# Four row tiles of the last chunk of K in seven products, and the product units one place earlier

## The chip, the core and the metric

The kernel runs on one core of a Trainium2 chip. The core has a matrix engine (TensorE, PE in the profile, with its weight loads as PEld), a vector engine (DVE), a scalar engine (ACT), GpSimd (POOL), SyncE (SP), and 16 DMA engines that bring data from HBM. Measured is the device time of the one launch in microseconds (us).

## The reference

Two layers of an encoder over 256 positions of width 2048, in float32. Layer 0 mixes by pooling and grouped-query attention, layer 1 by an mLSTM; these parts are not touched. Behind each stands a gated feed-forward part, in which the change lies:

```python
def conv_ffn(x, w_up, conv_w, conv_b, w_down):      # D_FF = 5632
    u = x @ w_up                                     # 2048 -> 2 * 5632
    up = jnp.pad(u, ((0, 0), (1, 1), (0, 0)))
    u = c[0] * up[:, :-2] + c[1] * up[:, 1:-1] + c[2] * up[:, 2:] + conv_b
    gate, val = jnp.split(u, 2, axis=-1)
    return (jax.nn.silu(gate) * val) @ w_down        # 5632 -> 2048
...
    x = x + conv_ffn(rms_norm(x, norm_ffn[layer]), w_up[layer], conv_w[layer], conv_b[layer], w_down[layer])
```

## The kernel before

**Numbers.** Every float32 operand of a product is split in a high part, rounded to the matrix engine's fp32r type, and a low part that holds the rest. A product of two tiles is three matmuls: high by high, high by low, low by high (`product`, `mov_part`).

**Weights.** `Stream` feeds them in the order in which TensorE uses them. A tile of 128 x 1024 (512 KB) is loaded by SP into one of six buffers w; ACT casts its high part (L127) and DVE subtracts for the low part (L128), both into one of four buffers hl. A tile of hl serves 12 matmuls of a direct product, six of the seven-product kind, 16 of the up-projection. Some weights of the seven products are sums of two blocks: SP loads one, POOL adds the other by DMA (L109 to L113, tile sum, prepared up to ten tiles ahead), and a third is made by DVE from a load and that sum (L123, L124).

**Up.** The hidden width of 5632 is 44 tiles. `up` makes one tile of gate and one of value in 64 matmuls, and then: ACT copies out of PSUM (L427) and DVE adds (L428, tb_up), DVE multiplies by the norm (L984), ACT forms three terms of the convolution for each of the two (L989 to L991), DVE adds them (L992, L993), ACT takes the silu (L997), DVE multiplies (L998, tile s), ACT and DVE split the result into g (L999, L1000).

**Down.** K, the 5632 rows, goes in six chunks of 4, 8, 8, 8, 8 and 8 row tiles. The 2048 columns are four blocks of 512; blocks 0 and 1 are the first half (h = 0), 2 and 3 the second (h = 1). In all chunks but the last, two row tiles, two position tiles and the two blocks of a half are a 2 x 2 block product that is made in seven products in place of eight. For this, `combine` ("mix" in the plan) makes, for pair j of chunk c, three combinations of s into s3 and a fourth into s1: DVE steps L1006, L1007, L1008 (tile sf), then ACT casts (L1012) and DVE subtracts (L1013). Unit A takes four of the products (three with s3, one with g), unit B the other three (two with g, one with s1); a unit of two pairs has 24 or 18 matmuls (pp). `drain` adds a unit's sums out of PSUM to acc and x (L1068), and `total` finishes a half in eight adds (L1085) when its last unit is in. In layer 0, chunk 1 takes the seven products in the second half alone, pair by pair, and goes directly in the first.

The last chunk goes directly (dn, end): `down_two` takes blocks 0 and 1, row tiles 0 to 5 of both and then 6 and 7 of both; `down` takes blocks 2 and 3, in layer 1 the last of them in `down_end`. DVE adds each block to x (L437, L1114). In layer 0 each finished block goes to the next norm (`nxt.add`), whose transposes (xt, L315) open the mixer of layer 1; in layer 1 it goes out.

**Order.** TensorE's order is written by hand: `_ffn_plan` lists ups, units, mixes and downs, and each unit stands between two ups. DVE, ACT, POOL and SP have an order that the scheduling layer sets when the program is built; on the chip each works its own list in order. In the names below up1_36 is tile 36 of layer 1, the first of its chunk 5; s31_4_3 is s3 of layer 1, chunk 4, pair 3. Chunk c's units of both halves follow the ups of chunk c + 1:

```python
        if halves == (0, 1):
            slots = [[(kind, c - 1, h, js)] for h in (1, 0) for kind in "AB"
                     for js in ((0, 1), (2, 3))[: pairs // 2]]
...
        for i in range(n):
            seq.append(("up", c, i))
            seq += slots[i] if i < len(slots) else []
```

Of the kernel before, what the change touches and what calls it, by code (L numbers as in the profile page):

```python
# [16 lines left out]
P = 128  # L17
# [192 lines left out]
def trunk(ctx: ExitStack, tc: tile.TileContext, gx, xT, xn, call, catt, cml, weights, mixes, out):  # L210
# [749 lines left out]
    def ffn_layer(layer, norm, nxt):  # L960
        with ExitStack() as es:
# [7 lines left out]
            combos, pss, quads, seen = {}, {}, {}, set()  # L969
# [86 lines left out]
            def drain(kind, c, h, order):  # L1056

                x00, x01, x10, _ = parts_of_x(h)
                if kind == "A":
                    steps = [(acc[:, h, k], v.tensor_add, e) for k, e in enumerate(order[:3])]  # L1060
                    steps.append((x10, v.tensor_add, 3))
                else:
                    steps = [(acc[:, h, 3], v.tensor_add, 0), (x00, v.tensor_add, 1), (x01, v.tensor_sub, 2)]
                for to, op, e in steps:
                    if e in (4, 6, 5, 0) and (kind, h) not in seen:
                        a.copy(to, pss[e])
                    else:
                        tc.keep_in_program_order(op(to, to, pss[e]))  # L1068
# [47 lines left out]

            def down(c, b):
                gt, last = gts[c], c == len(FCH) - 1
                kts = list(range(FCH[c]))
                if last and nxt is None and b == NB - 1:  # L1120
                    down_end(gt, b, kts)
                    return
# [7 lines left out]
                elif last:  # L1130
                    nxt.add(b)

            def down_two(c):

                gt, n = gts[c], FCH[c]
                pss2 = [mmp.tile([P, 2, 512], F32, tag="mm", name=f"dn{layer}_{c}_{b}") for b in range(2)]
                for kts in (range(n - 2), range(n - 2, n)):
                    for ps in pss2:
                        mov_part(ps, lambda k: gt[:, k], list(kts), kts[0] == 0, kts[-1] == n - 1)
                wv.until(lambda: ("A", 0) not in seen or ("total", 0) in pss)  # L1140
                for b, ps in enumerate(pss2):
# [8 lines left out]
            for kind, c, i, *j in _ffn_plan(layer):  # L1150
# [7 lines left out]
                elif kind == "down":  # L1158
                    down(c, i)
                elif kind == "two":  # L1160
                    down_two(c)
# [23 lines left out]
def _mov(w):  # L1185

    return w.reshape(-1, 2, P, 512).transpose(0, 2, 1, 3).reshape(-1, P, CH * P)
# [38 lines left out]

def _halves(layer, c):

    return () if c in (-1, len(FCH) - 1) else (0, 1) if c in BOTH[layer] else (1,)


def _ffn_plan(layer):

    seq = []
    for c, n in enumerate(FCH):
        pairs = FCH[c - 1] // 2 if c else 0  # L1240
        halves = _halves(layer, c - 1)

        if halves == (0, 1):
            slots = [[(kind, c - 1, h, js)] for h in (1, 0) for kind in "AB"
                     for js in ((0, 1), (2, 3))[: pairs // 2]]
            slots = [[]] * (pairs < 4) + slots
        else:
            slots = [[(kind, c - 1, 1, (j,))] for kind in "AB" for j in range(pairs)]
            for b in range(2 if pairs else 0):
                slots[(b + 1) * pairs // 2 - 1].append(("down", c - 1, b))  # L1250

        busy = {j: k for k, slot in enumerate(slots) for u in slot if u[0] == "A" for j in u[3]}
        for i in range(n):
            seq.append(("up", c, i))
            seq += slots[i] if i < len(slots) else []
            if c < len(FCH) - 1:
                seq += [("mix", c, j) for j in range(n // 2) if i == max(2 * j + 1, busy.get(j, 0))]
    return seq + [("two", len(FCH) - 1, 0)] + [("down", len(FCH) - 1, b) for b in range(2, NB)]


def _down_chunks(layer, w):
# [2 lines left out]
    out, k0 = [], 0  # L1264
    for c, n in enumerate(FCH):
        rows = w[k0 * P : (k0 + n) * P]
        blocks = [_mov(rows[:, b * 512 : b * 512 + 512]) for b in range(NB) if b // 2 not in _halves(layer, c)]
# [18 lines left out]
def _ffn_weights(layer, up, parts):  # L1286
# [3 lines left out]
    for kind, c, i, *j in _ffn_plan(layer):  # L1290
# [1 line left out]
            out += up[u : u + 4]  # L1292
            u += 4
        elif kind in ("down", "two"):
            out += [next(down) for _ in range(FCH[c] // 2 * (2 if kind == "two" else 1))]
# [119 lines left out]
```

## Time and profile before

| | |
|---|---|
| time, median of 3 runs | 2163.98 us (2162.7 to 2164.5) |
| the profiled execution | 2163.78 us, span 2162.0 us |
| granted TensorE clock | 1.00 |
| DMA moved | 555.29 MB, mean 257 GB/s |
| largest groups of DVE and ACT | L128, 840 times, 1009.4 us; L127, 839 times, 863.4 us |
| up | 5632 matmuls, 994.0 us busy |
| pp, the seven products | 1428 matmuls |
| dn and end, direct | 480 matmuls |

The span is the time from the first to the last instruction of the program; the time of the execution holds 1.8 us more. The groups' lines are those of the listing; a helper such as `mm` (L264) records all matmuls under one line, so they are told apart by their tiles.

### The profile page before, as it was taken

The page shows a single profiled execution, that of the slowest core. Times are in us where ns is not written, and L with a number is a line of the kernel's source. Part 1 is how long each engine was busy: PE and PEld are TensorE (multiplying, and loading weights), DVE is VectorE, ACT ScalarE, POOL GpSimd, SP SyncE. Part 2 cuts the span into 40 slices and gives each one's busy share as a digit, 9 for nine tenths or more (in the row PEclk, how much of TensorE's full clock was granted, in tenths as well). Part 3 has the DMA queues.
Part 4 walks back from the last instruction along what each step waited for, and adds up shares of the span by engine and source line. Part 5 has one row for each costly group of instructions (what it writes and reads, how often), then busy time and mean ns, then how long its engine had stood idle before and what let it go on. Part 6 is the DMA issues. An engine that isn't in the chain of part 4 may idle for free.

```text
span 2162.0 us, 31902 instructions
## 1 busy us (share of the span) xinstructions
PE 2156.2 (100%) x11412; PEld 1844.2 (85%) x11412; DVE 1734.7 (80%) x2425; ACT 1414.3 (65%) x2208; POOL 212.7 (10%) x268
## 2 busy tenths in 40 slices
PE   9999999999999999999999999999999999999999
PEld 7888888888888888889888888888888888888887
DVE  7686688887988988986777676667889898988896
ACT  7665578766777767666454544457777777776763
POOL 0022111110100100001111111211100000000000
PEclk9999999999999999999999999999999999999999
DMA  9668989898999877779888888898978787887774
GB/s 323 213 202 250 287 250 311 248 280 247 298 296 293 287 257 232 266 232 252 231 246 251 237 250 230 273 276 249 289 226 285 258 283 246 265 262 251 233 249 162
DMA packets 164097, 555.29 MB, mean 257 GB/s; under 512 B 20602, under 2 KB 23202, under 8 KB 163938
## 3 DMA queue, kind: packets, MB, share of 16 engines
q1 hardware_dynamic: 129632, 462.88, 62.0%
q0 software_dynamic: 20704, 52.71, 14.8%
q10 hardware_dynamic: 13602, 37.67, 5.7%
q8 instruction: 89, 1.46, 0.3%
q14 instruction: 70, 0.57, 0.1%
HBM read 551.04 MB, written 69.25 MB: 287 GB/s over the span
## 4 chain that ended last, share of the span: by engine, by line
PE 97%; DVE 2%; DMA 1%; issue 0%; ACT 0%; DVEq 0%
PE up L264 44%; PE pp L264 15%; PE op L264 8%; PE dn L264 5%; PE mv L264 4%; PE mq L264 4%; PE mk L264 4%; PE mo L264 4%; PE qproj L264 3%; PE kproj L264 1%; PE vproj L264 1%; PE pool L264 1%; DVE hl L128 1%; PE qk L264 1%; PE av L264 1%; PE end L264 1%
## 5 line engine op out<-in xcount | busy, mean ns | idle before, releaser
L128 DVE TENSOR_TENSOR hl<-w,hl 128x1024 fp32r<-128x1024 f32 (+2 forms) x840 | 1009.4, 1214 | 218.4 <-ACT hl L127 216.0
L127 ACT CAST hl<-w 128x1024 fp32r<-128x1024 f32 (+2 forms) x839 | 863.4, 1047 | 451.4 <-PE up L264 145.3
L264 PE MATMUL up<-xx,hl 128*128 128x512 f32 (+1 forms) x5632 | 994.0, 337 | 0.0
L264 PEld LDWEIGHTS up<-xx,hl 128*128 128x128 f32 x5632 | 866.9, 188 | 130.9 <-DVE hl L128 0.5
L264 PE MATMUL pp<-hl,s 128*128 128x512 f32 x816 | 204.9, 392 | 0.3 <-DVE hl L128 0.3
L264 PEld LDWEIGHTS pp<-hl,s 128*128 128x128 f32 x816 | 150.4, 188 | 32.0 <-DVE hl L128 1.2
L473 POOL DMA_DIRECT2D m<-m x128 | 102.1, 800 | 701.0 <-PE up L264 293.1
L264 PE MATMUL pp<-hl,g 128*128 128x512 f32 x612 | 156.9, 391 | 0.0
L427 ACT COPY tb_up<-up 128x512 f32<-128x512 f32 x88 | 51.6, 587 | 123.4 <-PE up L264 123.2
L264 PEld LDWEIGHTS pp<-hl,g 128*128 128x128 f32 x612 | 112.2, 188 | 22.3
L991 ACT ACTIVATE y<-tb_up,conv 128x256 f32<-128x256 f32 x176 | 104.4, 593 | 0.0
L992 DVE TENSOR_TENSOR y<-y,z 128x510 f32<-128x510 f32 x88 | 60.7, 689 | 52.2 <-ACT y L991 52.2
L473 POOL DMA_DIRECT2D m<-in_dn x64 | 54.6, 853 | 468.1 <-PE dn L264 168.1
L264 PE MATMUL dn<-hl,g 128*128 128x512 f32 x432 | 100.3, 391 | 0.0
L428 DVE TENSOR_TENSOR tb_up<-up,tb_up 128x512 f32<-128x512 f32 x88 | 60.8, 691 | 49.2 <-ACT tb_up L427 48.9
L264 PEld LDWEIGHTS dn<-hl,g 128*128 128x128 f32 x432 | 80.6, 188 | 16.6
L989 ACT ACTIVATE z<-tb_up,conv 128x256 f32<-128x256 f32 x176 | 88.9, 505 | 5.1 <-DVE tb_up L984 4.2
L264 PE MATMUL mk<-xx,hl 128*128 128x512 f32 (+1 forms) x512 | 92.2, 337 | 0.0
L264 PE MATMUL mq<-xx,hl 128*128 128x512 f32 (+1 forms) x512 | 92.1, 337 | 0.0
L264 PE MATMUL mv<-hl,xx 128*128 128x512 f32 (+2 forms) x480 | 91.7, 350 | 0.0
L264 PE MATMUL op<-hl,cat 128*128 128x512 f32 x384 | 91.6, 393 | 0.0
L264 PE MATMUL mo<-hl,xx 128*128 128x512 f32 x384 | 90.5, 391 | 0.0
(232 smaller groups left out, 2196.5 us busy)
## 6 DMA issues: line engine op xcount, KB each, us to landing
w<-in_up SPq DMA_DIRECT2D x352, 512.0 KB, 4.8
w<-in_dn SPq DMA_DIRECT2D x176, 512.0 KB, 4.6
w<-in_m_in SPq DMA_DIRECT2D x124, 512.0 KB, 5.1
m<-in_dn ACTq DMA_DIRECT2D x128, 256.0 KB, 5.5
w<-m SPq DMA_DIRECT2D x64, 512.0 KB, 5.0
w<-in_a_in SPq DMA_DIRECT2D x46, 512.0 KB, 5.3
sum<-in_dn SPq DMA_DIRECT2D x36, 512.0 KB, 5.4
sum<-in_dn POOLq DMA_DIRECT2D x36, 512.0 KB, 9.1
```

The lines of the kernel that those rows point to most:

```text
L127: (self.nc.vector.tensor_copy if i + c == 0 else self.nc.scalar.copy)(hl[:, 0, c : c + n], w[:, c : c + n])
L128: low = self.nc.vector.tensor_sub(hl[:, 1, c : c + n], w[:, c : c + n], hl[:, 0, c : c + n].bitcast(F32))
L264: last_mm[0] = pe.matmul(out_, lhsT, rhs, start=start, stop=stop, skip_group_check=True)
L427: a.copy(tb, ps[:, :, 1, :])
L428: v.tensor_add(tb, ps[:, :, 0, :], tb)
L473: paced(eng.dma_start(to[p : p + P // 2], src[p : p + P // 2], **kw))
L989: a.activation(z[:, 0, j, :], u[:, j, :], AF.Copy, scale=cw(tl, 0))
L991: a.activation(y[:, j, :], u[:, j, :], AF.Identity, scale=cw(tl, 1), bias=cw(tl, 3))
L992: v.tensor_add(y[:, :, 1:S], y[:, :, 1:S], z[:, 0, :, 0 : S - 1])
```

## The change

The last chunk now puts row tiles 0 to 3 of the second half through seven products as well (LAST = 4 in both layers): one A unit and one B unit of two pairs. Blocks 2 and 3 keep row tiles 4 to 7 as direct products. The A unit follows the chunk's last up; `down_two` is called in two parts, and the B unit stands between them. The second half's `total` follows that B unit, in place of the B unit of chunk 4. And the units of chunks 1 to 4 start one place earlier: the first A unit of a chunk stands after the chunk's own last up, in place of after the first up of the next.

```diff
+LAST = (4, 4)
...
-                n = FCH[c] // 2
+                n = _pairs(layer, c)
...
-                if kind == "B" and c == len(FCH) - 2:
+                if kind == "B" and c == _last_chunk(layer, h):
                     wv.add(total(h), 1.5)
...
-                kts = list(range(FCH[c]))
+                kts = list(range(_direct(layer, c, b), FCH[c]))
...
-            def down_two(c):
+            def down_two(c, second):
 
                 gt, n = gts[c], FCH[c]
-                pss2 = [mmp.tile([P, 2, 512], F32, tag="mm", name=f"dn{layer}_{c}_{b}") for b in range(2)]
-                for kts in (range(n - 2), range(n - 2, n)):
-                    for ps in pss2:
-                        mov_part(ps, lambda k: gt[:, k], list(kts), kts[0] == 0, kts[-1] == n - 1)
+                if not second:
+                    twos.extend(mmp.tile([P, 2, 512], F32, tag="mm", name=f"dn{layer}_{c}_{b}") for b in range(2))
+                parts = [(ps, kts) for kts in (range(n - 2), range(n - 2, n)) for ps in twos]
+                for ps, kts in parts[1:] if second else parts[:1]:
+                    mov_part(ps, lambda k: gt[:, k], list(kts), kts[0] == 0, kts[-1] == n - 1)
+                if not second:
+                    return
...
+def _pairs(layer, c):
+
+    return (LAST[layer] if c == len(FCH) - 1 else FCH[c]) // 2
+
+
+def _last_chunk(layer, h):
+
+    return len(FCH) - (1 if h and LAST[layer] else 2)
+
+
+def _direct(layer, c, b):
+
+    return LAST[layer] if c == len(FCH) - 1 and b >= NB // 2 else 0
...
+    slots = [[] for _ in range(FT)]
+    for c in range(len(FCH)):
+        pairs, halves = _pairs(layer, c), _halves(layer, c)
+
+        at = sum(FCH[: c + 1]) + (1 if pairs < 4 else -1)
+        if c == len(FCH) - 1:
+            at = FT - 1
+            ends = [(kind, c, 1, tuple(range(pairs))) for kind in "AB" if pairs]
+            slots[at] += ends[:1]
+        elif halves == (0, 1):
+            for h in (1, 0):
+                for kind in "AB":
+                    for js in ((0, 1), (2, 3))[: pairs // 2]:
+                        slots[at].append((kind, c, h, js))
+                        at += 1
...
+            seq += slots[f0 + i]
+            seq += [("mix", c, j) for j in range(_pairs(layer, c))
+                    if i == max(2 * j + 1, busy.get((c - 1, j), 0) - f0)]
+        f0 += n
+    seq += [("two", c, 0)] + ends[1:] + [("two", c, 1)]
+    return seq + [("down", c, b) for b in range(2, NB)]
...
-    n = sum(FCH[:-1]) // 2
+    n = (sum(FCH[:-1]) + LAST[layer]) // 2
```

The lines of the changed program stand one lower: L428 is now L429, L1013 is L1014.

DVE's list in layer 1, where chunk 4 ends and chunk 5 begins, before: up1_36 is the first up of chunk 5, sf1_4_3 and s31_4_3 are the combinations of the last pair of chunk 4.

```order
L1006 TENSOR_TENSOR sf1_4_3_18788<-s1_34_18607 128x256
L428 TENSOR_TENSOR tb_up1_36_18890<-up1_36_18799,tb_up1_36_18890 128x512
L1000 TENSOR_TENSOR g1_4_17581<-s1_34_18607,g1_4_17581 128x256
L128 TENSOR_TENSOR hl805_18931<-w805_18843,hl805_18931 128x1024
L1007 TENSOR_TENSOR sf1_4_3_18788<-sf1_4_3_18788,s1_34_18607 128x128
L984 TENSOR_TENSOR tb_up1_36_18890<-tb_up1_36_18890,R3_13695 128x512
L128 TENSOR_TENSOR hl806_18942<-w806_18867,hl806_18942 128x1024
L128 TENSOR_TENSOR hl807_18951<-w807_18913,hl807_18951 128x1024
L123 TENSOR_TENSOR w811_18961<-w811_18961,sum810_18864 128x512
L1008 TENSOR_TENSOR sf1_4_3_18788<-sf1_4_3_18788,s1_34_18607 128x128
L128 TENSOR_TENSOR hl808_18963<-w808_18927,hl808_18963 128x1024
L1013 TENSOR_TENSOR s31_4_3_18792<-sf1_4_3_18788,s31_4_3_18792 128x384
```

And in the changed program, up to the same combination:

```order
L129 TENSOR_TENSOR hl811_19011<-sum811_18858,hl811_19011 128x1024
L1007 TENSOR_TENSOR sf1_4_3_18894<-s1_34_18695 128x256
L1001 TENSOR_TENSOR g1_4_17687<-s1_34_18695,g1_4_17687 128x256
L429 TENSOR_TENSOR tb_up1_36_18990<-up1_36_18905,tb_up1_36_18990 128x512
L1008 TENSOR_TENSOR sf1_4_3_18894<-sf1_4_3_18894,s1_34_18695 128x128
L129 TENSOR_TENSOR hl812_19024<-w812_18946,hl812_19024 128x1024
L985 TENSOR_TENSOR tb_up1_36_18990<-tb_up1_36_18990,R3_13742 128x512
L1009 TENSOR_TENSOR sf1_4_3_18894<-sf1_4_3_18894,s1_34_18695 128x128
L129 TENSOR_TENSOR hl813_19035<-w813_18967,hl813_19035 128x1024
L1014 TENSOR_TENSOR s31_4_3_18898<-sf1_4_3_18894,s31_4_3_18898 128x384
```

The three sf rows and the row that writes s31_4_3 stand nearer to tb_up1_36, the first sf ahead of it.

TensorE's list in layer 1, where s31_4_3 is first used, before (pp1_4_14 to 13 are the four sums of unit A in PSUM):

```order
L264 MATMUL up1_37_18960<-xx3_9301,hl809_18982 128x256 x2
L264 MATMUL pp1_4_14_18909<-hl810_19003,s31_4_2_18498 128x512 x3
L264 MATMUL pp1_4_16_18910<-hl810_19003,s31_4_2_18498 128x512 x3
L264 MATMUL pp1_4_15_18911<-hl811_19026,s31_4_2_18498 128x512 x3
L264 MATMUL pp1_4_13_18912<-hl811_19026,g1_4_17581 128x512 x3
L264 MATMUL pp1_4_14_18909<-hl812_19065,s31_4_3_18792 128x512 x3
L264 MATMUL pp1_4_16_18910<-hl812_19065,s31_4_3_18792 128x512 x3
L264 MATMUL pp1_4_15_18911<-hl813_19078,s31_4_3_18792 128x512 x3
L264 MATMUL pp1_4_13_18912<-hl813_19078,g1_4_17581 128x512 x3
```

and now:

```order
L265 MATMUL up1_36_18905<-xx3_9349,hl808_18927 128x256 x2
L265 MATMUL pp1_4_14_18843<-hl809_18948,s31_4_2_18587 128x512 x3
L265 MATMUL pp1_4_16_18844<-hl809_18948,s31_4_2_18587 128x512 x3
L265 MATMUL pp1_4_15_18845<-hl810_18971,s31_4_2_18587 128x512 x3
L265 MATMUL pp1_4_13_18846<-hl810_18971,g1_4_17687 128x512 x3
L265 MATMUL pp1_4_14_18843<-hl811_19011,s31_4_3_18898 128x512 x3
L265 MATMUL pp1_4_16_18844<-hl811_19011,s31_4_3_18898 128x512 x3
L265 MATMUL pp1_4_15_18845<-hl812_19024,s31_4_3_18898 128x512 x3
L265 MATMUL pp1_4_13_18846<-hl812_19024,g1_4_17687 128x512 x3
```

The same unit stood behind up1_37, the second up of chunk 5; it now stands behind up1_36.

DVE's list in layer 0, where chunk 2 ends and chunk 3 begins (up0_20 is the first up of chunk 3), the last twelve rows up to the combination of the last pair before:

```order
L984 TENSOR_TENSOR tb_up0_20_5362<-tb_up0_20_5362,R1_2582 128x512
L128 TENSOR_TENSOR hl207_5423<-w207_5385,hl207_5423 128x1024
L123 TENSOR_TENSOR w211_5433<-w211_5433,sum210_5336 128x512
L1007 TENSOR_TENSOR sf0_2_3_5258<-sf0_2_3_5258,s0_18_5103 128x128
L128 TENSOR_TENSOR hl208_5435<-w208_5399,hl208_5435 128x1024
L128 TENSOR_TENSOR hl209_5455<-w209_5412,hl209_5455 128x1024
L123 TENSOR_TENSOR w213_5474<-w213_5474,sum212_5396 128x512
L124 TENSOR_TENSOR w211_5433<-w211_5433 128x512
L1008 TENSOR_TENSOR sf0_2_3_5258<-sf0_2_3_5258,s0_18_5103 128x128
L992 TENSOR_TENSOR y0_20_5366<-y0_20_5366,z0_20_5367 128x2x255
L128 TENSOR_TENSOR hl210_5476<-sum210_5336,hl210_5476 128x1024
L1013 TENSOR_TENSOR s30_2_3_5262<-sf0_2_3_5258,s30_2_3_5262 128x384
```

and in the changed program, from tb_up0_20 to the same combination:

```order
L429 TENSOR_TENSOR tb_up0_20_5413<-up0_20_5327,tb_up0_20_5413 128x512
L1007 TENSOR_TENSOR sf0_2_3_5316<-s0_18_5128 128x256
L129 TENSOR_TENSOR hl209_5447<-w209_5369,hl209_5447 128x1024
L985 TENSOR_TENSOR tb_up0_20_5413<-tb_up0_20_5413,R1_2582 128x512
L1001 TENSOR_TENSOR g0_2_4074<-s0_18_5128,g0_2_4074 128x256
L1008 TENSOR_TENSOR sf0_2_3_5316<-sf0_2_3_5316,s0_18_5128 128x128
L129 TENSOR_TENSOR hl210_5459<-w210_5390,hl210_5459 128x1024
L129 TENSOR_TENSOR hl211_5470<-w211_5432,hl211_5470 128x1024
L1009 TENSOR_TENSOR sf0_2_3_5316<-sf0_2_3_5316,s0_18_5128 128x128
L993 TENSOR_TENSOR y0_20_5417<-y0_20_5417,z0_20_5418 128x2x255
L1014 TENSOR_TENSOR s30_2_3_5320<-sf0_2_3_5316,s30_2_3_5320 128x384
```

The combination's rows stand nearer to tb_up0_20, and all of them behind it; the first convolution sum of up0_20 (y0_20) stands among them.

TensorE's list at the end of layer 1 in the changed program, from the last products of unit A, which follows the last up (up1_43), to the second direct block:

```order
L265 MATMUL pp1_5_15_20051<-hl864_20069,s31_5_1_19503 128x512 x3
L265 MATMUL pp1_5_13_20052<-hl864_20069,g1_5_18904 128x512 x3
L265 MATMUL dn1_5_0_20103<-hl865_20081,g1_5_18904 128x512 x12
L265 MATMUL dn1_5_0_20103<-hl866_20093,g1_5_18904 128x512 x12
L265 MATMUL dn1_5_0_20103<-hl867_20107,g1_5_18904 128x512 x12
L265 MATMUL pp1_5_10_20162<-hl868_20126,g1_5_18904 128x512 x3
L265 MATMUL pp1_5_11_20163<-hl868_20126,g1_5_18904 128x512 x3
L265 MATMUL pp1_5_10_20162<-hl869_20145,g1_5_18904 128x512 x3
L265 MATMUL pp1_5_11_20163<-hl869_20145,g1_5_18904 128x512 x3
L265 MATMUL pp1_5_12_20164<-hl870_20167,s11_5_0_19494 128x512 x3
L265 MATMUL pp1_5_12_20164<-hl870_20167,s11_5_1_19504 128x512 x3
L265 MATMUL dn1_5_1_20104<-hl871_20178,g1_5_18904 128x512 x12
```

Before, the B unit of chunk 4 (pp1_4_00 to 02) stood behind up1_43, and the direct blocks dn1_5_0 and dn1_5_1 followed it without a unit between them.

More of the change, by code (lines that the diff above doesn't have):

```diff
@@ L1227, in _halves @@
 def _halves(layer, c):
-    return () if c in (-1, len(FCH) - 1) else (0, 1) if c in BOTH[layer] else (1,)
-def _ffn_plan(layer):
-    seq = []
-    for c, n in enumerate(FCH):
[L1240 to L1252, printed above, removed]
+    return () if c == len(FCH) - 1 else (0, 1) if c in BOTH[layer] else (1,)
@@ L1253, in _ffn_plan @@
         for i in range(n):
             seq.append(("up", c, i))
[L1255 to L1258, printed above, removed]
+            seq += slots[f0 + i]
+            seq += [("mix", c, j) for j in range(_pairs(layer, c))
+                    if i == max(2 * j + 1, busy.get((c - 1, j), 0) - f0)]
@@ L1266, in _down_chunks @@
         rows = w[k0 * P : (k0 + n) * P]
-        blocks = [_mov(rows[:, b * 512 : b * 512 + 512]) for b in range(NB) if b // 2 not in _halves(layer, c)]
+        blocks = [_mov(rows[_direct(layer, c, b) * P :, b * 512 : b * 512 + 512]) for b in range(NB) if b // 2 not in _halves(layer, c)]
         if c == len(FCH) - 1:
@@ L1294, in _ffn_weights @@
         elif kind in ("down", "two"):
-            out += [next(down) for _ in range(FCH[c] // 2 * (2 if kind == "two" else 1))]
+            n = FCH[c] // 2 - 1
+            out += [next(down) for _ in range((n, n + 2)[i] if kind == "two" else (FCH[c] - _direct(layer, c, i)) // 2)]
         elif kind != "mix":
```

14 lines of the change are left out of this document (11 added, 3 removed).

## The prediction

> **What bounds the kernel now.** I read the page's totals first, then the waits of TensorE, then TensorE's own timeline where chunks meet.
>
> ```profile
> PE 2156.2 (100%) x11412; PEld 1844.2 (85%) x11412; DVE 1734.7 (80%) x2425; ACT 1414.3 (65%) x2208; POOL 212.7 (10%) x268
> PE 97%; DVE 2%; DMA 1%; issue 0%; ACT 0%; DVEq 0%
> ```
>
> The first line is busy time by engine, the second the chain that ended last by engine: TensorE holds both. Busy time of a pipelined engine proves little, so the view of its waits follows, all of them.
>
> ```profile
> PE wps L288 <- DVE pad L682: 1.2, 1, 1.2
> PE pp L264 <- DVE hl L128: 0.3, 1, 0.3
> PE ptr L587 <- ACT pr L578: 0.2, 1, 0.2
> PE tr_q L546 <- DVE rot_q L514: 0.2, 1, 0.2
> ```
>
> It waits 1.9 us in 2162. And it runs at its rate: the timeline of PE at the last chunk boundary of the second layer (start, length, what) shows equal work taking equal time.
>
> ```profile
> 1986.93 11.30 PE L264 MATMUL up<-xx,hl 128*128 128x512 f32 x64
> 1998.07 2.24 PE L264 MATMUL pp<-hl,s 128*128 128x512 f32 x9
> ...
> 2003.60 11.30 PE L264 MATMUL up<-xx,hl 128*128 128x512 f32 x64
> 2014.74 1.55 PE L264 MATMUL pp<-hl,s 128*128 128x512 f32 x6
> ```
>
> From start to start an up takes 1998.07 − 1986.93 = 11.14 us and an A unit of 24 products' matmuls 2003.60 − 1998.07 = 5.53 us, 0.230 us a matmul. Time that is taken off TensorE comes off the end, and a wait that is put on it is added to the end: nothing else in the program has slack to give it back.
>
> [...]
>
> ```profile
> L264 PEld LDWEIGHTS pp<-hl,s 128*128 128x128 f32 x816 | 150.4, 188 | 32.0 <-DVE hl L128 1.2
> ```
>
> [...] I take no slack in the sum.
>
> **The products themselves.** The last rows of the chain of waits give the price of both kinds.
>
> ```profile
> 2095.38 4.11 PE pp L264 x18
> 2099.48 11.13 PE up L264 x64
> 2110.62 4.11 PE pp L264 x18
> 2114.72 32.64 PE dn L264 x144
> 2147.36 10.89 PE end L264 x48
> ```
>
> In a layer 48 direct matmuls go (two pairs of row tiles, two column blocks) and one A unit of 24 and one B unit of 18 come. Direct: 32.64 / 144 = 0.2267 us each; A: 0.2304; B: 4.11 / 18 = 0.2283. Both layers: 96 × 0.2267 = 21.8 us go, 48 × 0.2304 + 36 × 0.2283 = 19.3 us come. That is **−2.5 us**, and it is the most that the change can gain: 0.12%.
>
> **The units one place ahead.** A unit's third and fourth pair use combinations (s3) of the last four up tiles of their chunk. Before, the A unit of pairs 2 and 3 came after the second up of the next chunk, with the A unit of pairs 0 and 1 ahead of that up; now it comes straight after the first up. Seen from the end of that first up, the use moves forward by one A unit and one up, 5.53 + 11.14 = 16.67 us. DVE's timeline at that boundary of the kernel before tells when the combination is ready.
>
> ```profile
> 1998.80 0.42 DVE L1006 TENSOR_TENSOR sf<-s 128x256 f32<-128x256 f32 x1
> 1999.13 0.68 DVE L428 TENSOR_TENSOR tb_up<-up,tb_up 128x512 f32<-128x512 f32 x1
> 1999.73 0.41 DVE L1000 TENSOR_TENSOR g<-s,g 128x256 fp32r<-128x256 f32 x1
> 2000.14 1.23 DVE L128 TENSOR_TENSOR hl<-w,hl 128x1024 fp32r<-128x1024 f32 x1
> 2001.29 0.28 DVE L1007 TENSOR_TENSOR sf<-sf,s 128x128 f32<-128x128 f32 x1
> 2001.49 0.68 DVE L984 TENSOR_TENSOR tb_up<-tb_up,R 128x512 f32<-128x512 f32 x1
> 2002.09 2.35 DVE L128 TENSOR_TENSOR hl<-w,hl 128x1024 fp32r<-128x1024 f32 x2
> ...
> 2004.97 0.28 DVE L1008 TENSOR_TENSOR sf<-sf,s 128x128 f32<-128x128 f32 x1
> 2005.17 1.22 DVE L128 TENSOR_TENSOR hl<-w,hl 128x1024 fp32r<-128x1024 f32 x1
> 2006.31 0.55 DVE L1013 TENSOR_TENSOR s<-sf,s 128x384 fp32r<-128x384 f32 x1
> ```
>
> It ends at 2006.86, 8.79 us after the up's end (1998.07). It is used in the unit that starts at 2014.74, from its 13th matmul (2.77 us in) by its high part and from the 15th, at +3.23 us, by the low part that this row writes: 11.1 us to spare. With the use 16.67 us earlier, a combination that stayed where it is would be 8.79 − 3.23 = 5.56 us late.
>
> It does not quite stay. In the changed order of DVE the three steps of the combination stand earlier, yet the last two or three still stand behind tb_up of that same up, in five boundaries in one order: tb_up, sf, hl, tb_up, sf, hl, s. Nothing of it can start before ACT has copied the up out of PSUM:
>
> ```profile
> 1998.27 0.59 ACT L427 COPY tb_up<-up 128x512 f32<-128x512 f32 x1 [1.70 <-PE up L264]
> 1998.75 0.41 ACT L999 CAST g<-s 128x256 fp32r<-128x256 f32 x1
> 1999.06 3.08 ACT L127 CAST hl<-w 128x1024 fp32r<-128x1024 f32 x3
> ...
> 2003.37 0.51 ACT L1012 CAST s<-sf 128x384 fp32r<-128x384 f32 x1
> 2003.78 0.51 ACT L989 ACTIVATE z<-tb_up,conv 128x256 f32<-128x256 f32 x1
> ...
> 2005.89 0.60 ACT L991 ACTIVATE y<-tb_up,conv 128x256 f32<-128x256 f32 x1
> ```
>
> Counted from the up's end: the copy ends at 1998.27 + 0.59 − 1998.07 = +0.79, DVE's tb_up starts at about +0.82 and holds it 0.60 (1999.13 to 1999.73), sf 0.20 (2001.29 to 2001.49): +1.62. The hl needs its cast, which follows the copy on ACT (3.08 / 3 = 1.03): it starts at +1.80, holds 1.15: +2.95. tb_up 0.60, sf 0.20, the second hl 1.14, then s 0.55: +5.44. The 15th matmul would start at +3.23: **2.2 us of wait at each of five boundaries** (layer 0 into chunks 4 and 5, layer 1 into 3, 4 and 5). The high part, cast by ACT after the second sf (+3.75, 0.51), comes at about +4.3 and only moves where within the 2.2 us the wait sits.
>
> The two other boundaries have orders of their own. In layer 1 into chunk 2 the last sf stands ahead of the hl, which waits for its cast anyway: 1.80 + 1.14 + 0.60 + 1.14 + 0.55 = +5.23, **2.0 us**. In layer 0 into chunk 3 all three sf, three hl, a g and the first convolution sum of the same up stand between tb_up and s. DVE comes to that sum at 1.42 + 0.33 (sf), hl from 1.80 to 2.95, + 0.60 + 0.41 + 0.20 + 1.14 + 1.14 + 0.20 = +6.6; ACT's six conv steps last 2005.89 + 0.60 − 2003.78 = 2.71 and start after the cast of the fourth hl, which waits for the second tile of the unit (+2.77, + 1.03): +6.5. So 6.6 + 0.60 + 0.55 = +7.8, **4.6 us**. Layer 0 into chunk 2 takes single pairs with two ups between: no wait. Together 5 × 2.2 + 2.0 + 4.6 = **+17.6 us**. What is late next is ACT's and DVE's next hl, which TensorE's wait gives time to come; I add nothing for it.
>
> Bounds for one boundary: 1.5 us if the cast of the hl is done before DVE asks and the short steps cost nothing; 5.56 us if the combination ends as late as it does now. I take 2.2, since the new rows are known and each has a duration.
>
> **The tail of each layer.** DVE gets work at the place where it must also split weights fastest. Its groups by form give the lengths:
>
> ```profile
> L128 DVE TENSOR_TENSOR hl<-w,hl 128x1024 fp32r<-128x1024 f32 x826 | 998.5, 1221 | 213.7 <-ACT hl L127 211.3
> L1068 DVE TENSOR_TENSOR acc<-acc,pp 128x512 f32<-128x512 f32 x60 | 39.6, 680 | 0.0
> L123 DVE TENSOR_TENSOR w<-w,sum 128x512 f32<-128x512 f32 x36 | 24.7, 686 | 7.0 <-DMA w<-in_dn 7.0
> L1085 DVE TENSOR_TENSOR x<-x,acc 128x512 f32<-128x512 f32 x24 | 16.1, 686 | 0.0
> ```
>
> and the windows of busy time its load there: the stretch after the last up of layer 1, then of layer 0 (PE, weight loads, DVE, ACT, POOL, then clock and DMA share).
>
> ```profile
> 2110.50:2153.00 42.50, 42.50 (x190) 35.19 (x189) 32.42 (x39) 20.18 (x25) 0.00 (x0) 1.00 0.52 174
> 925.40:972.00 46.60, 46.60 (x219) 38.62 (x218) 38.10 (x55) 27.84 (x47) 1.90 (x3) 1.00 0.73 236
> ```
>
> A layer's end gains seven tiles of split weights for four, 3 × 1.14; four sums of chained weights and seven drains of products, 11 × 0.60; and the eight steps of the second half's total move into it, 8 × 0.60: 14.8 us on top of 32.4, in a tail of 186 matmuls, some 42 us. DVE is then full there. In layer 1, from tb_up of the last up to the first split tile of the second direct block, DVE has 8 splits, 13 rows of 512 and one g: 8 × 1.14 + 13 × 0.60 + 0.41 = 17.3 us from +0.82, while TensorE asks for that tile at 5.53 + 36 × 0.2267 + 4.11 = +17.8. That is 0.3 us late if DVE arrives on time, and about 1.8 if the rows ahead of it (a chained sum, a split that waits for its buffer, an x) hold it 1.5 us: I take 1.3. Layer 0 the same, and 0.6 for the hand-over, where the transposes of the third block wait behind eight rows of the first two. **+3.2 us**, bounds 0 and 7.
>
> The DMA issues grow by three tiles a layer on SP (two of them first halves of sums) and two on POOL (their second halves). The units' stream is only shifted against the ups, the DMA share in that tail is 0.52, and the one group that waits for weights (L123, 7.0 us in 36) did so without TensorE waiting as long: nothing added. The ten combination steps a layer that are new on DVE fall between ups of the last chunk, ahead of its end, under TensorE's work.
>
> **Sum.** On the profiled execution, 2163.8 us with a span of 2162.0: −2.5 + 17.6 + 3.2 = +18.3, so 2182 us. Its own time is 0.2 us below the median of the runs shown; that shift is left out.
>
> **Rivals.**
>
> 1. The combinations come in time and only the products count: 2163.8 − 2.5 = 2161 us, not slower. It decides if s ends within 3.23 us of the up's end. For it speaks that the kernel before had 11.1 us to spare; against it that tb_up, two splits and s alone hold DVE 0.60 + 1.15 + 1.14 + 0.55 = 3.4 us, from +0.82. Chance 0.05.
> 2. The wait is there but about 1 us a place, because DVE and ACT run these rows closer than I laid them: 2163.8 − 2.5 + 7 + 2 = 2170 us. Chance 0.10.
> 3. DVE arrives late at tb_up at each boundary, since it is 80% busy over the span and more here, and s ends where it does now: 2163.8 − 2.5 + 7 × 5.56 + 3.2 = 2203 us. For it: before, DVE took tb_up at +1.06, not +0.82. Against: rows that stood ahead of it there have moved. Chance 0.10.
> 4. The stalls cost clock besides: if after each one the 10 matmuls left of the unit ran at half the rate, 10 × 0.23 = 2.3 us more at seven places: 2198 us. In the profile the clock stands at 1.00 in every window above, where TensorE never stops. Chance 0.04.
> 5. TensorE has slack of its own and takes the waits up: 2161 us again. Against: up and A units take the same 11.14 and 5.53 us wherever they stand, and no row shows them faster. Chance 0.01.
>
> [...]
>
> **How the numbers follow.** The forecast, 2182 us, has 0.70. About what a measurement of this kernel tells from no change is 0.2%, 4.3 us. A gain above it is beyond the −2.5 us: 0.01. Within it lie rivals 1 and 5 and a small part of rival 2: 0.07. Slower: the rest, 0.92. The forecast's own bounds are 2163.8 − 2.5 + 7 × 1.5 = 2172 and 2163.8 − 2.5 + 17.6 + 7 × 1.0 + 7 = 2193; the range is 2171 to 2194, which leaves out rivals 1, 3, 4 and 5 and the lower part of rival 2.
>
> **What would show it.** TensorE's waits should list pp waiting for s (the combination's subtraction) about seven times, 2 to 2.5 us each and one nearer 5, in the A unit after the first up of a chunk; the A unit of pairs 0 and 1 should still take 5.53 us; DVE should be over 90% busy after each layer's last up. Matmuls of dn, end and pp together should be 12 fewer. A time under 2168 would say that DVE took the combination well ahead of tb_up's tail; waits for hl instead of s, or a lower clock, that my place for the loss is wrong.

## The result, and the profile after

The changed kernel takes 2193.57 us (median of 4 executions, 2191.07 to 2197.41) against 2163.66 us for the kernel before on the same chip: ratio 1.014, with an interval of 95% from 1.0124 to 1.0156. It is slower by 30 us, where 18 were forecast. The profiled execution is the fastest of the four, 2191.07 us with a span of 2189.3 us: 27.3 us over that of before. Its granted clock is 0.997; the two slowest of the four show 0.995 and 0.996, and the section on the hardware says what that costs. The points below are reckoned in the profiled execution.

The page after, busy time by engine and the chain that ended last:

```profile
PE 2164.4 (99%) x11400; PEld 1844.6 (84%) x11400; DVE 1764.8 (81%) x2473; ACT 1421.0 (65%) x2222; POOL 214.6 (10%) x272
PE 91%; DVE 6%; issue 1%; DMA 1%; ACT 0%; ACTq 0%; SPq 0%; DVEq 0%; POOLq 0%
```

The 12 matmuls that should go are gone. But PE's busy time has risen by 8 us with 12 matmuls fewer (some matmuls run slower, as the windows below show), and DVE now holds 6% of the chain. The waits of TensorE (us in total, times, longest) say for what; three others, 1.6 us together, are the first, third and fourth of the list before:

```profile
PE pp L265 <- DVE s L1014: 9.2, 6, 1.6
PE pp L265 <- ACT s L1013: 6.5, 7, 4.7
PE pp L265 <- DVE hl L129: 1.6, 4, 0.6
PE xt L316 <- DVE x L438: 1.1, 1, 1.1
PE dn L265 <- DVE hl L129: 0.7, 1, 0.7
```

L1014 and L1013 are the subtraction and the cast of the combination, one line further down than before. The first two rows are the seven boundaries, the last three the tails of the layers. One boundary, layer 1 into chunk 5, on TensorE's timeline:

```profile
2027.61 2.24 PE L265 MATMUL pp<-hl,s 128*128 128x512 f32 x9
...
2030.75 0.73 PE L265 MATMUL pp<-hl,s 128*128 128x512 f32 x2 [0.21 <-ACT s L1013]
2033.07 1.88 PE L265 MATMUL pp<-hl,s 128*128 128x512 f32 x7 [1.58 <-DVE s L1014]
2034.78 0.86 PE L265 MATMUL pp<-hl,g 128*128 128x512 f32 x3
2035.48 1.78 PE L265 MATMUL up<-xx,hl 128*128 128x512 f32 x9
```

and on DVE's:

```profile
2028.43 0.69 DVE L429 TENSOR_TENSOR tb_up<-up,tb_up 128x512 f32<-128x512 f32 x1 [0.43 <-ACT tb_up L428]
2029.04 0.28 DVE L1008 TENSOR_TENSOR sf<-sf,s 128x128 f32<-128x128 f32 x1
2029.38 1.23 DVE L129 TENSOR_TENSOR hl<-w,hl 128x1024 fp32r<-128x1024 f32 x1
2030.52 0.69 DVE L985 TENSOR_TENSOR tb_up<-tb_up,R 128x512 f32<-128x512 f32 x1
2031.12 0.28 DVE L1009 TENSOR_TENSOR sf<-sf,s 128x128 f32<-128x128 f32 x1
2031.32 1.22 DVE L129 TENSOR_TENSOR hl<-w,hl 128x1024 fp32r<-128x1024 f32 x1
2032.46 0.55 DVE L1014 TENSOR_TENSOR s<-sf,s 128x384 fp32r<-128x384 f32 x1
```

The row at 2032.46 ends at 2033.01, 5.40 us after the up's end (2027.61); +5.44 was forecast. TensorE goes on at 2033.07, and the A unit takes 2035.48 − 2027.61 = 7.87 us in place of 5.53. Measured in this way, from its start to the start of the next up, the seven units are:

| layer, into chunk | unit, us | over 5.53 | wait forecast | clock in the window |
|---|---|---|---|---|
| 0, 3 | 12.89 | 7.36 | 4.6 | 0.79 |
| 0, 4 | 8.27 | 2.74 | 2.2 | 1.00 |
| 0, 5 | 9.01 | 3.48 | 2.2 | 0.89 |
| 1, 2 | 7.67 | 2.14 | 2.0 | 1.00 |
| 1, 3 | 9.19 | 3.66 | 2.2 | 0.86 |
| 1, 4 | 7.87 | 2.34 | 2.2 | 1.00 |
| 1, 5 | 7.87 | 2.34 | 2.2 | 1.00 |

Where the clock stays at 1.00 the excess is the forecast wait and 0.1 to 0.5 us. At three places it is more, and the windows (stretch, its length and PE busy, clock, DMA share and GB/s) show why:

```profile
558.00:574.00 16.00, 11.27 (x44) 0.79 1.04 340
823.00:838.00 15.00, 13.20 (x58) 0.89 0.88 288
1766.00:1778.00 12.00, 10.21 (x41) 0.86 0.98 300
```

A clock of 0.86 is the mean of the window: the clock is 0.50 in a part of it (in the third from 1772.37 to 1775.79), called half clock here, and 1.00 in the rest. The third window on TensorE's timeline, layer 1 into chunk 3:

```profile
1771.54 2.66 PE L265 MATMUL pp<-hl,s 128*128 128x512 f32 x7 [1.58 <-DVE s L1014]
1774.00 1.48 PE L265 MATMUL pp<-hl,g 128*128 128x512 f32 x3
```

After the same wait of 1.58 us the last three matmuls take 1.48 us here and 0.86 at the boundary into chunk 5: 0.2 us more each. Such a stretch costs 1.6 us (1.32 of this unit over the 7.87 of its neighbours, and 0.25 of the up behind it, 11.39 for 11.14). After the long wait, in layer 0 into chunk 3, it costs more:

```profile
565.87 4.31 PE L265 MATMUL pp<-hl,s 128*128 128x512 f32 x9 [4.73 <-ACT s L1013]
569.98 1.28 PE L265 MATMUL pp<-hl,g 128*128 128x512 f32 x3
571.10 5.28 PE L265 MATMUL up<-xx,hl 128*128 128x512 f32 x29
```

Twelve matmuls from 565.87 to 571.10 are 5.23 us in place of 12 × 0.2304 = 2.76: 2.5 us. This wait ended with ACT and not with DVE: ACT's cast of the combination ran at 565.32, although its input (L1008) was done at 563.23, because ACT's list has six convolution steps of the up ahead of it (L990 to L992, 562.73 to 565.42).

### The profile page after: what moved, and what is told of

Read it like the earlier page. It is cut to its first block, busy times and chain, and to the rows that moved or that the text cites. A ratio compares the mean times of both kernels' runs of the same rounds, so it can differ in the third digit from the quotient of the medians.

```text
span 2189.3 us, 31993 instructions
## 1 busy us (share of the span) xinstructions
PE 2164.4 (99%) x11400; PEld 1844.6 (84%) x11400; DVE 1764.8 (81%) x2473; ACT 1421.0 (65%) x2222; POOL 214.6 (10%) x272
## 4 chain that ended last, share of the span: by engine, by line
PE 91%; DVE 6%; issue 1%; DMA 1%; ACT 0%; ACTq 0%; SPq 0%; DVEq 0%; POOLq 0%
PE up L265 42%; PE pp L265 13%; PE op L265 8%; PE mv L265 4%; PE mq L265 4%; PE mk L265 4%; PE mo L265 4%; PE qproj L265 3%; PE dn L265 3%; DVE hl L129 2%; DMA sum<-in_dn 1%; PE vproj L265 1%; PE kproj L265 1%; PE pool L265 1%; PE qk L265 1%
## 5 line engine op out<-in xcount | busy, mean ns | idle before, releaser
L129 DVE TENSOR_TENSOR hl<-w,hl 128x1024 fp32r<-128x1024 f32 (+1 forms) x842 | 1010.7, 1214 | 219.9 <-ACT hl L128 217.1
L265 PE MATMUL pp<-hl,s 128*128 128x512 f32 x864 | 223.2, 399 | 17.3 <-DVE s L1014 9.2
L265 PEld LDWEIGHTS pp<-hl,s 128*128 128x128 f32 x864 | 159.8, 190 | 56.9 <-DVE s L1014 12.2
L265 PE MATMUL pp<-hl,g 128*128 128x512 f32 x648 | 167.8, 394 | 0.0
L265 PEld LDWEIGHTS pp<-hl,g 128*128 128x128 f32 x648 | 120.2, 190 | 24.2
L428 ACT COPY tb_up<-up 128x512 f32<-128x512 f32 x88 | 51.5, 585 | 120.7 <-PE up L265 120.6
L992 ACT ACTIVATE y<-tb_up,conv 128x256 f32<-128x256 f32 x176 | 103.9, 591 | 0.0
L429 DVE TENSOR_TENSOR tb_up<-up,tb_up 128x512 f32<-128x512 f32 x88 | 60.8, 691 | 50.5 <-ACT tb_up L428 50.3
L990 ACT ACTIVATE z<-tb_up,conv 128x256 f32<-128x256 f32 x176 | 88.5, 503 | 5.4 <-DVE tb_up L985 4.8
L265 PE MATMUL op<-hl,mcat 128*128 128x512 f32 x384 | 89.5, 392 | 0.0
L265 PEld LDWEIGHTS mq<-xx,hl 128*128 128x128 f32 x512 | 79.2, 188 | 11.6
```

Source lines behind the costliest of these rows:

```text
L129: low = self.nc.vector.tensor_sub(hl[:, 1, c : c + n], w[:, c : c + n], hl[:, 0, c : c + n].bitcast(F32))
L265: last_mm[0] = pe.matmul(out_, lhsT, rhs, start=start, stop=stop, skip_group_check=True)
L428: a.copy(tb, ps[:, :, 1, :])
L429: v.tensor_add(tb, ps[:, :, 0, :], tb)
L990: a.activation(z[:, 0, j, :], u[:, j, :], AF.Copy, scale=cw(tl, 0))
L992: a.activation(y[:, j, :], u[:, j, :], AF.Identity, scale=cw(tl, 1), bias=cw(tl, 3))
```

## The experiments

E1 to e4 were compared with the kernel before at 2163.78 us, e5 to e7 at 2163.41, e8 at 2163.9.

| run | what differs | us | ratio to before, interval |
|---|---|---|---|
| e1_place_back | units at their old place | 2169.31 | 1.0023 (1.0014 to 1.0032) |
| e2_place_alone | no last-chunk units | 2186.55 | 1.0106 (1.0092 to 1.0119) |
| e3_mend | combination ahead of tb_up | 2181.28 | 1.0081 (1.0067 to 1.0095) |
| e4_fill | eight matmuls in each wait | 2189.47 | 1.0117 (1.0103 to 1.0131) |
| e5_mend_hl | and ahead of a split | 2173.52 | 1.0047 (1.0034 to 1.006) |
| e6_last_early | and last units earlier | 2169.81 | 1.003 (1.0019 to 1.0041) |
| e7_longer | longer waits | 2211.34 | 1.0221 (1.0206 to 1.0237) |
| e8_split_first | e6, tb_up behind that split | 2166.43 | 1.0011 (1.0002 to 1.002) |

**The two halves of the change.**

```diff
-        at = sum(FCH[: c + 1]) + (1 if pairs < 4 else -1)
+        at = sum(FCH[: c + 1]) + (1 if pairs < 4 else 0)
```

> Units of chunks of four pairs at the place they had before (the A unit of pairs 2 and 3 behind the second up of the next chunk), the last chunk still in seven products. Theory (nearly the whole loss is the place: seven waits for the combination, some 18.5 us, and the half clock behind some of them, some 5 us): no wait of pp for s, clock 1.000, and the time is before's 2163.7 minus 2.5 for the products plus the tails (5.2 measured in the changed kernel) plus what the last chunk's A unit waits for banks behind the B unit that now stands right ahead of it, 0 to 3 us a layer: 2166 to 2173. Rival (the loss comes from the last chunk's products and the fuller tails): the time stays above 2185.

2169.31 us, as the theory had it. No row of the waits names s any more; they are the last chunk's A unit, which now stands right behind the B unit of chunk 4 and waits for its banks to be drained, and the tail:

```profile
PE pp L265 <- DVE acc L1069: 2.6, 4, 0.7
PE xt L316 <- DVE x L438: 1.6, 1, 1.6
PE pp L265 <- DVE x L1069: 1.3, 2, 0.7
```

```diff
-LAST = (4, 4)
+LAST = (0, 0)
```

> The units one place ahead, and the last chunk wholly direct as before (no last-chunk units, no row tile of it in seven products). Theory: the seven waits of the changed kernel and its half clock come back whole, and no tail: 2163.7 + 18.5 + 5 = 2187 (2184 to 2190), waits of pp for s about 18 us in the profile, clock 0.995 to 0.998. Rival (the waits need the last chunk's extra work on DVE): under 2175.

2186.55 us, 0.5 from the forecast of this run. The waits are those of the changed kernel, to 0.2 us:

```profile
PE pp L265 <- DVE s L1014: 9.4, 6, 1.7
PE pp L265 <- ACT s L1013: 6.4, 7, 4.6
```

So the place alone costs 22.8 us of the 30 (2186.55 − 2163.78), and the last chunk's products, though they take matmuls away, some 6 in either company: 2193.57 − 2186.55 = 7.0 with the place, 2169.31 − 2163.78 = 5.5 without it.

**Is it DVE's order, or its load?** Two order-only edges were set, with no data in them:

```diff
-        a.copy(tb, ps[:, :, 1, :])
-        v.tensor_add(tb, ps[:, :, 0, :], tb)
+        one = a.copy(tb, ps[:, :, 1, :])
+        two = v.tensor_add(tb, ps[:, :, 0, :], tb)
+        if after:
+            behind(one, after[0])
+            behind(two, after[1])
```

Here `after` holds the cast and the subtraction into s3 of the last combination.

> The changed kernel with one order more: the cast and the subtraction of the fourth pair's combination stand ahead of ACT's copy and DVE's tb_up of the next chunk's first up. Theory (the combination is ready to be made before that up ends, and only its place behind tb_up makes it late): s ends by about +2.8 us after the up's end, against 3.23 when it is used; the seven waits shrink below 0.5 us each, the clock is 1.000, and the time is 2163.7 - 2.5 + 5.2 = 2166.5 (2164 to 2171). Rival (DVE is full there and the combination comes as late from any place, behind the splits): waits of 1 to 2 us stay, 2174 to 2185.

2181.28 us: the theory was missed by 15, and the rival's range held. DVE's timeline at the boundary of layer 1 into chunk 5, where the up ends at 2020.35:

```profile
2021.68 1.23 DVE L129 TENSOR_TENSOR hl<-w,hl 128x1024 fp32r<-128x1024 f32 x1 [0.65 <-ACT hl L128]
2022.82 0.28 DVE L1012 TENSOR_TENSOR sf<-sf,s 128x128 f32<-128x128 f32 x1
2023.07 1.23 DVE L129 TENSOR_TENSOR hl<-w,hl 128x1024 fp32r<-128x1024 f32 x1
2024.21 0.55 DVE L1017 TENSOR_TENSOR s<-sf,s 128x384 fp32r<-128x384 f32 x1
```

tb_up is gone from ahead of s, and s still ends 2024.76 − 2020.35 = 4.4 us after the up's end, because the scheduling layer left two splits ahead of it. Those cannot start before TensorE gives their buffers back, the first at the up's end and the second 1.4 us later. So the row that holds the combination back need not be a long one: it is enough that it waits for TensorE itself. The next run sets the first of these splits behind the combination.

```diff
             low = self.nc.vector.tensor_sub(
                 hl[:, 1, c : c + n], w[:, c : c + n], hl[:, 0, c : c + n].bitcast(F32))
+            if self.hold and i == self.hold[0]:
+                self.behind(high, self.hold[1])
+                self.behind(low, self.hold[2])
```

`hold` names the unit's fourth weight tile, and the cast and the subtraction into s3.

> The mended order of the run before it, and the split of the unit's fourth weight tile behind the combination too. In the first mend DVE had two splits ahead of the subtraction, and these waited for buffers that TensorE frees at the up's end and 1.4 us later; s ended 3.9 us after the up's end. Theory (the waits are an order of DVE and nothing else): with both splits behind it the combination ends about 1.7 us after the up's end against 3.23 when it is used; no wait of pp for s above 0.3 us, clock 1.000, and only products and tails are left: 2163.7 - 2.5 + 5.2 = 2166.4 (2164 to 2169). Rival (the work displaced waits in its place: the fourth tile's split or tb_up comes late): waits of pp for hl of some 1 us at each of seven places, 2173.

(By the row shown above, s had ended 4.4 us after the up's end, not the 3.9 named here.) 2173.52 us, 7 over the theory. s is off the list but for 0.6 us, and something else is on it:

```profile
PE pp L269 <- DVE hl L130: 5.8, 8, 1.1
```

That is the rival: four of the eight are the tails' (1.6 us, as after the change), and at four boundaries the fourth tile's split is late in its turn, with two rows of tb_up ahead of it. With what stands around these waits the four units are 1.2 to 2.4 us over 5.53. The clock is 1.000. Three boundaries of layer 1 or 0 (into 2 and 5 in layer 1, into 5 in layer 0) have no excess left, so DVE's order, not its load, sets the wait there.

**The clock.** If half the clock is what TensorE's idle time costs, filling that time should bring it back. At the seven places eight matmuls with a stationary side of zeros were put ahead of the 13th; they add zero to the sum.

```diff
+                    if m == 4 and (kind, h, js) == ("A", 1, (2, 3)):
+                        for k in range(8):
+                            mm(pss[e], zero, hl[:, 0, 512:], False, False)
```

> The changed kernel with eight matmuls more ahead of the 13th matmul of the A unit of pairs 2 and 3, at the seven places that wait: their stationary side is zero, so they add nothing to the sum. TensorE is busy for 8 x 0.23 = 1.83 us of each wait. Theory (the half clock comes from TensorE's idle time): the combination is used at the same moment as in the changed kernel, the waits of pp for s shrink from some 18 us to some 5, and the clock is 1.000 but for the longest wait: the time falls by the clock's loss, some 3 to 5 us, to 2187 to 2191. Rival A (the half clock is no result of the waits): the time stays at 2193.5, clock 0.995 to 0.997. Rival B (the waits end in their own time only if TensorE leaves a resource alone; eight matmuls are added whole): 2193.5 + 7 x 1.83 = 2206.

2189.47 us, within the theory's range: 56 matmuls more, and 4.1 us less than the changed kernel in the median, though the two intervals still overlap by 0.0007. The clock is 0.998 or 0.999 in all four executions, where the changed kernel's four show 0.995 to 0.997. Its windows at the places where the clock had fallen:

```profile
557.00:573.00 16.00, 12.58 (x46) 0.79 1.00 320
825.00:837.00 12.00, 10.99 (x54) 1.00 0.83 236
1766.00:1778.00 12.00, 11.75 (x57) 1.00 0.93 273
```

Six of seven places are at 1.00; the seventh still has a wait of 3.4 us. Rival B is out: 2206 was nowhere near. The opposite test makes the waits longer.

```diff
+                    for _ in range(2 if j == 3 and d is s3 else 1):
-                    v.tensor_sub(d[:, 1], e, d[:, 0].bitcast(F32))
+                        v.tensor_sub(d[:, 1], e, d[:, 0].bitcast(F32))
```

> The changed kernel with the low part of the fourth pair's combination subtracted twice (the same values again); the second subtraction stands behind one more split, so that each wait grows by about 1.14 + 0.5 = 1.7 us: from some 2.2 to 3.9 us at six places, from 4.9 to 6.6 at one, 12 us in all. Theory (half clock follows TensorE's idle time, and the longer the wait the surer): the clock falls at all seven places, about 12 matmuls at 0.2 us more each, 17 us in all against 5 in the changed kernel: 2193.5 + 12 + 8 to 12 = 2213 to 2218. Rival (it falls at the same few places whatever the wait's length): 2206.

2211.34 us, 2 under the theory's range and 5 over the rival's. The clock fell at all seven places: here are the windows of the four that had been at 1.00 with the shorter wait (layer 0 into 4, layer 1 into 2, 4 and 5):

```profile
696.00:712.00 16.00, 12.11 (x52) 0.89 1.04 347
1644.00:1660.00 16.00, 12.61 (x49) 0.79 1.00 300
1911.00:1927.00 16.00, 12.60 (x55) 0.89 0.98 299
2044.00:2060.00 16.00, 12.61 (x54) 0.89 0.85 270
```

and its waits for s are 20.1 and 8.1 us:

```profile
PE pp L265 <- DVE s L1015: 20.1, 7, 3.2
PE pp L265 <- ACT s L1013: 8.1, 7, 6.4
```

That is 28.2 − 15.7 = 12.5 us of wait more; with four more stretches of half clock at 1.6 us it makes 18.9 of the 20.5 us by which the span has grown (2209.8 − 2189.3).

**The tails.** On top of the mended order the last chunk's A unit was put behind the last but one up and its B unit behind the last; to free the place, the two last B units of chunk 4 stand together.

```diff
-            at = FT - 1
-            ends = [(kind, c, 1, tuple(range(pairs))) for kind in "AB" if pairs]
-            slots[at] += ends[:1]
+            slots[FT - 3] += slots[FT - 2]
+            slots[FT - 2], slots[FT - 1] = ([(kind, c, 1, tuple(range(pairs)))] for kind in "AB")
...
-    seq += [("two", c, 0)] + ends[1:] + [("two", c, 1)]
+    seq += [("two", c, 0), ("two", c, 1)]
```

> The same, and the last chunk's two units one up earlier each: its A unit behind the last but one up, its B unit behind the last up; for this the last B unit of chunk 4 stands right behind the one before it. Theory (the tails' 5.2 us are DVE's load behind the last up): the A unit's splits and drains go under the last up, some 4 of the 5.2 us go: 2163.7 - 2.5 + 1 = 2162 (2161 to 2164). Rival (two B units in a row want splits faster than DVE makes them, or drains still hold the second half's total behind the end): 2166 or more.

2169.81 us, 3.7 less than the run without it; the expected 2162 was missed. The waits of xt and dn are gone from the list and the two A and B units of the last chunk run at their rate, but the pair of B units takes 9.17 us in place of 36 × 0.2304 = 8.29 in each layer; that is the rival's first reason, and its range (2166 or more) held. The rest of the miss is the waits for the split at the boundaries, which I had counted as mended. There are four of them as in the run before, but not at the same places: into chunks 3, 4 and 5 in layer 0 and into 5 in layer 1 (units 2.5, 1.7, 2.2 and 1.3 us over 5.53), where the run before had its four into 3 and 4 of both layers. In layer 0 into chunk 5 (up's end 817.75) DVE shows how such a wait comes about:

```profile
813.98 0.69 DVE L125 TENSOR_TENSOR w<-w,sum 128x512 f32<-128x512 f32 x1 [2.66 <-DMA sum<-in_dn]
...
821.07 0.56 DVE L1021 TENSOR_TENSOR s<-sf,s 128x384 fp32r<-128x384 f32 x1 [0.25 <-ACT s L1020]
821.56 0.69 DVE L433 TENSOR_TENSOR tb_up<-up,tb_up 128x512 f32<-128x512 f32 x1
822.28 0.69 DVE L992 TENSOR_TENSOR tb_up<-tb_up,R 128x512 f32<-128x512 f32 x1
822.89 2.35 DVE L130 TENSOR_TENSOR hl<-w,hl 128x1024 fp32r<-128x1024 f32 x2
```

DVE stood 2.66 us for a sum's transfer shortly before the up's end, comes late to the combination, and then takes tb_up ahead of the split that TensorE wants next. The last run sets ACT's copy and DVE's tb_up behind that split:

```diff
                 self.behind(high, self.hold[1])
                 self.behind(low, self.hold[2])
+                self.behind(self.hold[3], high)
+                self.behind(self.hold[4], low)
```

> The run before last (mended order, last chunk's units one up earlier), with ACT's copy and DVE's tb_up of the next chunk's first up also behind the split of the unit's fourth weight tile. There the waits that were left (5.8 us of pp for hl, six times) came where two rows of tb_up stood between the combination and that split. Theory (DVE's order still sets these waits): each wait at a boundary shrinks by the 0.7 to 1.2 us of those rows, 4 of them almost to nothing; 2169.8 - 5 = 2165 (2163.5 to 2167), level with before or a little above. Rival (DVE comes late to the boundary anyway, in layer 0 from sums that wait for their transfer): 2168 or more. A time below before's 2163.4 by the whole 2.5 us of the products isn't expected, since the two B units in a row still cost 0.9 us a layer.

2166.43 us, within the theory's range. What is left of these waits is 4.0 us with that of the pair of B units, most of it in layer 0 into chunks 3 and 4 (units of 7.74 and 7.25 us, 2.2 and 1.7 over 5.53; the other five are less than 0.5 over):

```profile
PE pp L271 <- DVE hl L130: 2.3, 5, 0.7
PE pp L271 <- ACT s L1023: 1.7, 2, 1.1
```

Ahead of the boundary into chunk 3 DVE again stood for a sum's transfer, 2.78 us until 554.17, as the rival has it; whether another order would remove these last two waits was not tried. So 27.1 of the 30 us (2193.57 − 2166.43) came back, by the order of DVE and ACT and the place of the last chunk's units, with all other units still one place ahead. It is level with the kernel before to 0.11% (0.02 to 0.2%), and no version beat that kernel: the products can give 2.5 us at most, and the pair of B units alone takes 1.8 of them.

## Why the prediction was right, and where it was short

The path, the wait and the places are as predicted; the size is 30 us where 18 were forecast. That 2193.57 us lies inside the range (2171 to 2194) is in part luck: two of the four executions, 2194.98 and 2197.41, lie above it, and the upper end was reckoned from longer waits (7 us more) and tails of 7 us. The waits exceeded the forecast by 1.6 us and the tails by 2.3; the room that they left was filled by a term that stood at nothing, the clock.

- **TensorE sets the end, and has no slack.** Right. Every wait in the list came out in the time. Rival 5 is out. Not quite right is that A units took 5.53 us wherever they stood: two of the kernel before, in layer 0 into chunks 3 and 4, took 6.11 and 5.81, 0.9 us together.
- **The units one place ahead, +17.6.** Right. Seven waits for s at the seven places named, one near 5 us and the others at 2; the combination ended 5.40 us after the up where 5.44 was worked out. With what the half clock took of these units left out (2.5, 1.1 and 1.3 us), the table's excess is 24.1 − 4.9 = 19.2 us. E2 shows that it is the place: the same waits with nothing else changed. The largest error is 0.5 us, in layer 0 into chunk 4. In layer 0 into chunk 3 the size is near (4.9 for 4.6), but it was ACT's cast behind the convolution steps that ended the wait, where DVE's sum and subtraction had been laid out.
- **"The combinations come in time" (rival 1).** Not so in this program. But at five of the seven places the runs show the order of DVE and ACT and not their load: with the edges of e8 these units are within 0.5 us of 5.53. In layer 0 into chunks 3 and 4, where 2.2 and 1.7 us stay, load and transfers are not ruled out.
- **Waits that cost clock (rival 4).** This is the step that failed: I put 0 in the sum and 0.04 on the rival. It is half true: the clock fell at three of seven places, for 2.5 + 1.6 + 1.6 = 5.7 us in the profiled execution, where 2.3 at all seven was the rival's price. The row that I argued from, the clock of 1.00 before, could not speak of such a wait, for that kernel had none over 1.2 us.
- **The tails, +3.2.** Mis-sized: 5.5 us. In layer 0 the A unit lost 0.55, the B unit 0.84, dn 0.85 and xt 1.3; in layer 1 the A unit 0.48, the B unit 0.74 and dn twice 0.38. DVE is full there, as forecast (over 90%):

```profile
2140.90:2183.40 42.50, 41.65 (x181) 33.13 (x180) 40.06 (x53) 20.84 (x26) 0.00 (x0) 1.00 0.49 163
938.70:985.30 46.60, 43.98 (x201) 35.32 (x199) 44.03 (x62) 30.07 (x48) 1.58 (x2) 1.00 0.75 242
```

  It is busy for 94% of either (40.06 / 42.50, 44.03 / 46.60; third group of the row). I had looked only at the first split tile behind the B unit; the two units' own splits were late too, and the hand-over of x cost 1.3, not 0.6.
- **The products, −2.5.** Not measured alone. With it the terms come to −2.5 + 19.2 + 5.7 + 5.5 = 27.9; less the 0.9 us that the kernel before lost in its own two A units it is 27.0, against 27.3 measured in the profiled execution.
- **DMA, nothing.** At the seven places no wait of TensorE names a transfer. In e6 one delayed DVE, so it is not free where DVE has just become the next thing in the chain.

## What to carry to other kernels

When a consumer is moved ahead, look not only at when its input could be ready but at what the producing engine does in between: rows that themselves wait for the consumer (a copy out of its PSUM, a split into a buffer it frees) must not stand ahead of the input, and an order that was harmless with 11 us to spare is most of the loss without them. A wait of TensorE was paid for twice here where the clock fell behind it (1.6 us on top of some 2), so a few short waits are worth removing even where they look like a tenth of a per cent each. And a trade of matmuls for DVE rows belongs where DVE has time: here the same units one up earlier cost 3.7 us less.

## What the hardware showed that I had not expected

The clock fell to 0.50 behind waits for which I had put nothing in the sum. In the changed kernel's profiled execution two of the six waits of about 2 us (1.58 us of it in one piece in the row above) were followed by 3.4 us of matmuls 0.43 us apart in place of 0.23; in e2, with the same waits, one of six. In e7 all six waits with 3.2 us in one piece were, and the wait in layer 0 into chunk 3 (3.4 to 6.4 us in one piece) was in the changed kernel, e2, e4 and e7 alike. Waits of at most 1.1 us, which is all that e5, e6 and e8 had left at the boundaries and in the tails, kept the clock at 1.00.

In between, the length of the wait alone does not say which. The trace records the granted clock with its times. In the changed kernel it is 0.50 from 564.06 to 570.88, from 830.30 to 833.71 and from 1772.37 to 1775.79 (and at the program's end): 2, 1 and 1 times 3.413 us (the two single ones are 3.413 us in the record). The starts are 266.24 and 942.08 us apart, 78 and 276 times 3.413, so all these times lie on one grid of that step. The means of the windows of e2, e3, e4 and e7 agree with the step: 0.86 over 12 us and 0.89 over 16 are 3.4 and 3.5 us at 0.50, 0.79 over 16 is 6.7, and 0.72 over 18 is 10.1. Here are two stretches of this grid with a wait of about 2 us in them, each with the stretch behind it (its length, PE busy, clock, DMA share and GB/s), in layer 0 into chunk 5 and in layer 1 into chunk 2:

```profile
826.89:830.29 3.40, 1.80 (x7) 1.00 0.68 158
830.30:833.70 3.40, 3.40 (x10) 0.50 1.01 249
1639.27:1642.67 3.40, 1.82 (x7) 1.00 0.83 204
1642.68:1646.08 3.40, 3.40 (x20) 1.00 0.99 228
```

In the changed kernel's trace every stretch at full clock in which TensorE was busy for 1.80 us or less was followed by half clock (at the boundaries 0.49, 1.80 and 1.62 us), and none with 1.82 or more; a wait that the grid divides, as in layer 1 into chunk 5 (2.89 and 2.13 us busy), left the clock alone. This is one execution, and I read no general limit from it. The clock came back after a stretch that was busy throughout (from 567.47, 830.30 and 1772.37), and not after the one from 564.06, busy for 1.60 us. My reading is that the same wait costs clock or not by its place on the grid, and that the spread of the changed kernel, 6 us (clock 0.997 to 0.995) where the four executions of the kernel before keep within 2, goes with that place; the three executions that were not profiled do not show it.
